# Seven block products for eight in the up projection of a hybrid decoder layer

## The chip, the cores and the metric

The kernel runs on one core of a Trainium2 chip. The metric is the device time of one launch in microseconds. Engines are named as in the profile: PE (TensorE, matrix products), DVE (VectorE), ACT (ScalarE), POOL (GpSimd) and SP (which only issues DMAs here).

## The reference, cut to what matters

One decoder layer for 576 tokens: a prompt of 512 and eight sequences of 8 sample tokens. The width is 1024, the hidden width of the MLP 4096, all in float32.

```python
hn = rmsnorm(x, norm1_g)
proj = hn @ w_in                    # split between the two mixers
...                                 # gated DeltaNet (oa) and dilated attention (ob)
h1 = x + jnp.concatenate([oa, ob], axis=-1) @ w_o
hid = jnp.square(jax.nn.relu(rmsnorm(h1, norm2_g) @ w_up))
y = h1 + hid @ w_down
```

`rmsnorm` divides each token by the root of its mean square and multiplies by a gain per channel. The change concerns the last two lines and the residual that leads to them.

## The kernel before

Activations lie with channels on the 128 partitions and tokens along the free dimension, so the layer's input is 8 channel tiles of 576 tokens. The tokens are handled in two halves of 288.

**Products in two parts.** Each operand of a large product is split into a rounded value (`h`, in the type fp32r that PE takes at full rate) and a remainder (`l`). A product is then three: wh·xh, wh·xl and wl·xh, added in one PSUM bank. A weight chunk of 128 x 1024 is loaded (`wr`), ACT writes `wh`, and DVE subtracts to get `wl` (`splitter`, line 397).

**Stages.** First the attention projections, attention and delta rule run, interleaved. Then comes the output projection (`proj_o`, line 1532), in two halves of the contraction: the attention's half first (tile `mob`), then the delta heads' half (tile `moa`). For each of the 8 channel tiles `m` and each token half, `after_o` (line 1505) adds the result to the residual `h1`, writes `h1 * gain` in two parts (`h1h`, `h1l`) and squares it; POOL adds the squares up. When all squares are there, `stats2` sums them over the partitions with five small products into `ssum`, and spreads the scale of each token over the partitions (`row_bcast`: PE transposes into `rowb`, ACT copies out).

**MLP.** The blocks go in the order u0, u1, d0, u2, d1, ... u7, d6, d7. A block u makes 512 hidden channels: four row tiles, each a product over 8 channel tiles for both token halves. `relu2` takes it out of PSUM with two DVE operations (the token's scale is applied there, so the products don't wait for it), and splits the square in two parts (`hid`). A block d multiplies 512 hidden channels by w_down, and `add_down` adds each result to `h1`.

**What sets the order.** All of this is written as generators. `Flow` (line 91) merges them into one program order by a rough clock of its own for each engine; each engine then runs its instructions strictly in that order. What a generator needs is given by signals (`yield lambda: "delta" in done`) and by buffer classes with a limit (`get`, `rel`); the four classes share fixed numbers of tiles, `K` 13 of 1024 columns and `P` the 8 PSUM banks. `proj_o` and `mlp_gemm` are fillers: PE takes their next product whenever nothing else of PE's can start sooner.

Of the kernel before, what the change touches and what calls it, by code (L numbers as in the profile page):

```python
# [11 lines left out]
F32R = mybir.dt.float32r  # L12
# [5 lines left out]
NT = SEQ + NB * TS          # 576 tokens: the prompt, then the sample batches one after another  # L18
# [51 lines left out]
_GROUP = {"sb": "cs", "sbn": "cs", "pb": "cf"}     # the rest: "c"; parameters: "cp"  # L70
# [20 lines left out]
class Flow:  # L91
    """A list scheduler: merges generators into one program order, by a rough clock of each engine.
    A generator's instructions wait in its queue, and the one that can start first is issued.
    What a generator brings in one step is in order, and what follows a yield depends on it; one
    that fills has steps that depend on nothing but the times it is given. A generator yields a
    further delay, or a test that has to hold before its next step."""
# [4 lines left out]
    AHEAD = 4000      # how far loads that can wait may queue up  # L101
# [62 lines left out]
    def advance(self, c):  # L164
        """to the task's next instruction, if it has one yet"""
# [47 lines left out]
def hymba_step(ctx: ExitStack, tc: tile.TileContext, a):  # L213
# [5 lines left out]
    # a few classes of buffers, each shared by several uses; those that are held are counted, so  # L219
    # that none waits for a release that comes later in program order  # L220
# [36 lines left out]
    def mm(out, lhsT, rhs, start, stop, share=1):  # L257
        n = size(rhs) * (1 if rhs.dtype == F32R else 4)
        cost = max(n, size(lhsT) * (1 if rhs.dtype == F32R else 4)) / 2.4 + 3
# [63 lines left out]
    go_on = lambda t: None      # mark of what nothing in the generator waits for  # L323
# [13 lines left out]
    klass(kpool, "K", 13, {"wr": WR, "wh": 2, "wl": 2, "kv": 1, "es": 2, "so": 2, "ex": 3, "k": 13, "e": 2})  # L337
    klass(upool, "U", 16, {"st": 2, "nat": 7, "sq": 2, "cv": 4, "E": 1, "t": 6, "h1": 8, "rq": 4, "u": 16})
# [34 lines left out]
    for kind, c in order:  # L373
        for i in range(4):
            chunk[kind, c, i] = len(items)
            items.append((a["wu"][4 * c + i] if kind == "u" else a["wd"][c, i], 1024))
    raw = {}

    def load_w(i):
        src, cols = items[i]  # L380
        r = yield from get("wr", MID, "wr")
        dma(r[:, :cols], src, lambda t: raw.update({i: (r, t)}))
# [139 lines left out]
    # q and k of the prompt in two parts; the heads' outputs take the place of the lower parts  # L522
# [36 lines left out]
    def first_products(ps, n):  # L559
        """of the first chunk: each kind of product once its parts are there"""  # L560
# [340 lines left out]
    def gemm(wh, wl, x_h, x_l, nk, stride, off, after, need=None):  # L901
        """w^T x over nk tiles of the contraction, by halves of the tokens; after(half, psum) has
        the generator that takes a half away."""
        for hf, (c0, c1) in enumerate(HALF):
            p = yield from get("g", [128, 288], "pg")
            for j in range(nk):
                s = slice(j * stride + off, j * stride + off + 128)
                if need and need(j, hf) not in done:
                    yield lambda: need(j, hf) in done
                mm(p, wh[:, s], x_h[:, j, c0:c1], j == 0, False)  # L910
                mm(p, wh[:, s], x_l[:, j, c0:c1], False, False)
                mm(p, wl[:, s], x_h[:, j, c0:c1], False, j == nk - 1)
# [166 lines left out]
    def head_decay(h):  # L1079
        """the decay between tokens of a chunk, in either direction"""  # L1080
# [19 lines left out]
    def head_scores(h):  # L1100
        """k k^T and q k^T with the decay between tokens; the former goes to DRAM"""
# [70 lines left out]
    def head_tokens(h):  # L1172
        """k and v with tokens on partitions"""
# [40 lines left out]
    def substitution(nb, n, src, buf):  # L1214
        """Inverse of the unit lower triangular blocks src (one per partition), and its transpose."""
# [27 lines left out]
    def sub_prompt():  # L1243
# [16 lines left out]
        # the blocks of twice the size: a pair on two partitions, with half of the columns each  # L1260
# [222 lines left out]
    def after_delta():  # L1483
# [3 lines left out]
        rel("big")  # L1487
        cap.update(g=6, wr=4, wh=3, wl=3)
        sig("delta")

# [14 lines left out]
    def after_o(m, hf, p, last):  # L1505
# [9 lines left out]
        g = C["g2"][:, m:m + 1]  # L1515
        xh_ = hx["h"][:, m, c0:c1]
        yield 0
        act(xh_, x, scale=g)
        stt(hx["l"][:, m, c0:c1], x, g, f(xh_), OP.mult, OP.subtract)
        sig(("h1", m, hf))  # L1520
        yield 0
        acc = st2["acc"]
        if m:
            s = yield from get("t", [128, 288], "sq2")
            act(s, x, AF.Square)
            pool_tt(acc[:, c0:c1], acc[:, c0:c1], s, OP.add)
            rel("t")
        else:
            act(acc[:, c0:c1], x, AF.Square)
        sig(("sq", m, hf))  # L1530

    def proj_o():
        yield lambda: "prompt_attn" in done and "sample_attn" in done
        for kh in (1, 0):
            if kh:
                x = mob["t"]
            else:
                yield lambda: "delta" in done
# [11 lines left out]
        rel("big", "big")  # L1550
        sig("proj_o")
# [183 lines left out]
```

## Time and profile before

| | us |
|---|---|
| median of 3 runs | 830.47 |
| lowest and highest run | 829.9, 831.32 |
| span of the profiled execution, first to last instruction | 830.0 |

The profile is of one execution. Its page gives the span and no other time for that execution. Busy time of an engine is the time in which it executes an instruction. Lines such as L262 or L278 are helpers (`mm`, `tt`) through which all matrix products and all two-input DVE operations go, so the tiles tell them apart. A name before `<-` is what is written, those behind it are what is read.

### The profile page before, as it was taken

To read this page: it belongs to the slowest core of one execution; us is meant where nothing else is said; L and a number is where in the kernel's file an instruction comes from. 1 tells how busy PE (TensorE), PEld (TensorE's weight loads), DVE (VectorE), ACT (ScalarE), POOL (GpSimd) and SP (SyncE) were. 2 spreads that over 40 slices of the span, in tenths; PEclk is the share of its full clock that TensorE was granted. 3 is DMA by queue.
4 is the path that set the end of the run, shared out by engine and by line. 5 is a ranking of instruction groups with operands and counts; after the bars stand their busy time and mean duration, and the time that the engine had idled before them with its cause. 6 is when DMAs were issued, how large, how long until landed. Compare 5 with 4: busy or idle time off the path is not lost.

```text
span 830.0 us, 15794 instructions
## 1 busy us (share of the span) xinstructions
PE 811.8 (98%) x6486; PEld 750.2 (90%) x6486; DVE 506.3 (61%) x1126; ACT 283.8 (34%) x594; POOL 121.9 (15%) x140
## 2 busy tenths in 40 slices
PE   9989998999999999999999999999999999999998
PEld 9968877879778787789999999999999999999998
DVE  4366279788776885688756545546455554645552
ACT  5547454554332244442633212222132121222210
POOL 3443323134223000040520000000000000000000
PEclk9999999999999999999999999999999999999999
DMA  7722421016787896224223222222322232222102
GB/s 266 134 99 77 135 69 37 29 40 231 236 313 217 296 312 258 86 82 176 86 69 102 77 77 87 92 77 77 99 81 77 77 101 78 77 81 96 54 28 87
DMA packets 49863, 99.05 MB, mean 119 GB/s; under 512 B 12864, under 2 KB 26304, under 8 KB 49792
## 3 DMA queue, kind: packets, MB, share of 16 engines
q1 hardware_dynamic: 49792, 98.05, 35.9%
q8 instruction: 51, 0.84, 0.4%
q14 instruction: 20, 0.16, 0.1%
HBM read 88.15 MB, written 9.69 MB: 118 GB/s over the span
## 4 chain that ended last, share of the span: by engine, by line
PE 83%; DVE 8%; DMA 3%; ACT 3%; issue 1%; POOL 0%; SPq 0%; ACTq 0%; POOLq 0%
PE pg L262 61%; PE pa L262 8%; DVE y L285 3%; PE cha L262 2%; DMA wr<-in_wk_dram 1%; DMA morekv<-in_cv_dram 1%; PE ptp L265 1%; PE sn L262 1%; PE os L262 1%; PE sc L262 1%; PE cs L262 1%; PE py L262 1%; PE pv L262 1%; PE s L262 1%; ACT wh L270 1%
## 5 line engine op out<-in xcount | busy, mean ns | idle before, releaser
L262 PE MATMUL pg<-hid,wh 128*128 128x288 f32 x1024 | 203.7, 294 | 0.0
L262 PEld LDWEIGHTS pg<-hid,wh 128*128 128x128 f32 x1024 | 164.3, 188 | 0.0
L262 PE MATMUL pg<-h1h,wl 128*128 128x288 f32 x512 | 151.2, 295 | 0.0
L262 PE MATMUL pg<-hid,wl 128*128 128x288 f32 x512 | 151.2, 295 | 0.0
L262 PE MATMUL pg<-h1l,wh 128*128 128x288 f32 x512 | 150.9, 295 | 0.0
L262 PE MATMUL pg<-h1h,wh 128*128 128x288 f32 x512 | 150.7, 294 | 0.0
L270 ACT ACTIVATE wh<-wr 128x1024 fp32r<-128x1024 f32 (+1 forms) x104 | 105.7, 1017 | 110.2 <-PE pg L262 72.1
L278 DVE TENSOR_TENSOR h<-pg,h 128x288 f32<-128x288 f32 x160 | 72.9, 457 | 114.1 <-PE pg L262 114.1
L278 DVE TENSOR_TENSOR wl<-wr,wh 128x1024 fp32r<-128x1024 f32 (+1 forms) x89 | 107.1, 1203 | 16.2 <-ACT wh L270 16.0
L262 PEld LDWEIGHTS pg<-h1l,wh 128*128 128x128 f32 x512 | 96.1, 188 | 0.1
L262 PEld LDWEIGHTS pg<-h1h,wl 128*128 128x128 f32 x512 | 96.1, 188 | 0.0
L262 PEld LDWEIGHTS pg<-hid,wl 128*128 128x128 f32 x512 | 96.1, 188 | 0.0
L262 PEld LDWEIGHTS pg<-h1h,wh 128*128 128x128 f32 x512 | 96.1, 188 | 0.0
L270 ACT ACTIVATE hid<-rq 128x288 fp32r<-128x288 f32 x64 | 28.5, 445 | 181.5 <-DVE rq L285 181.5
L262 PE MATMUL pg<-xh,wh 128*128 128x288 f32 x256 | 78.3, 306 | 0.0
L262 PE MATMUL pg<-xh,wl 128*128 128x288 f32 x256 | 78.2, 305 | 0.0
L262 PE MATMUL pg<-xl,wh 128*128 128x288 f32 x256 | 78.1, 305 | 0.0
L285 DVE SCALAR_TENSOR_TENSOR rq<-pg,R2b 128x288 f32<-128x288 f32 x64 | 29.3, 458 | 68.4 <-PE pg L262 66.5
L262 PEld LDWEIGHTS pg<-xh,wh 128*128 128x128 f32 x256 | 48.6, 190 | 3.2 <-issue 3.0
L262 PEld LDWEIGHTS pg<-xh,wl 128*128 128x128 f32 x256 | 48.7, 190 | 2.8 <-issue 2.4
L262 PEld LDWEIGHTS pg<-xl,wh 128*128 128x128 f32 x256 | 48.7, 190 | 2.5 <-issue 1.8
L308 POOL TENSOR_TENSOR wl<-wr,wh 128x1024 fp32r<-128x1024 f32 x15 | 35.9, 2393 | 83.0 <-ACT wh L270 66.5
(281 smaller groups left out, 1331.2 us busy)
## 6 DMA issues: line engine op xcount, KB each, us to landing
wr<-in_wu_dram SPq DMA_DIRECT2D x32, 512.0 KB, 3.2
wr<-in_wd_dram SPq DMA_DIRECT2D x32, 512.0 KB, 3.3
morekv<-in_ck_dram SPq DMA_DIRECT2D x20, 512.0 KB, 4.9
morekv<-in_cv_dram SPq DMA_DIRECT2D x20, 512.0 KB, 5.8
wr<-in_wb_dram SPq DMA_DIRECT2D x16, 512.0 KB, 4.0
wr<-in_wo_dram SPq DMA_DIRECT2D x8, 512.0 KB, 5.5
xr<-in_xT_dram SPq DMA_DIRECT2D x8, 288.0 KB, 5.3
h<-in_xT_dram SPq DMA_DIRECT2D x8, 288.0 KB, 6.8
```

What stands on the lines that cost most here:

```text
L262: lambda: nc.tensor.matmul(out, lhsT, rhs, start=start, stop=stop, skip_group_check=True))
L265: fl.op("PE", (97, 230), lambda: nc.tensor.transpose(out, in_, ident[:k, :k]))
L270: fl.op("ACT", cost, lambda: nc.scalar.activation(out, in_, func, bias=bias, scale=scale, accum_out=accum), mark)
L278: dve(lambda: nc.vector.tensor_tensor(out, x, y, op=op), out, x, mark=mark)
L285: dve(lambda: nc.vector.scalar_tensor_tensor(out, x, s, y, op0=op0, op1=op1), out, x, 61 if ap(s) else 0, mark=mark)
L308: fl.op("POOL", 135 + size(x) / 0.47, lambda: nc.gpsimd.tensor_tensor(out, x, y, op=op), mark)
```

## The change

The product with w_up is made in blocks of 2 x 2: a unit is a pair of row tiles (256 hidden channels, 16 units in all), the contraction goes over four pairs of channel tiles, and the tokens are the two halves. A product of two 2 x 2 block matrices takes eight block products; written with sums of the blocks of either factor (Winograd's form of Strassen's scheme), it takes seven. Each of the seven has a PSUM bank of its own for the whole unit.

- Weights: a chunk now holds half the contraction of a pair of row tiles. POOL forms three sums (`ws`, 768 columns) and overwrites a quarter of the chunk by a fourth combination, in operations of 256 columns (`sums_splitter`). ACT and DVE then split both tiles in two parts (`two_parts`).
- Inputs: `after_o` writes `h1 * gain` in single precision into `xq`. POOL multiplies it by a scale S per token, from the first norm's variances, and forms four combinations (`x_factors`); ACT and DVE split the seven results (`x_parts`, tiles `xf`). S is spread by `token_scale`, and the second half of `proj_o` waits for it. The second norm's scale (`stats2`) divides S out again.
- Outputs: `up_out` forms the four blocks of the result from the seven banks, one operation on ACT and seven on DVE per unit, in `uq`; `up_square` applies the norm's scale, squares and splits.

`PO` is the order of the seven products; `OF_W` and `OF_X` name the factor of each. The long list of buffer limits is left out of the diff.

```diff
-            items.append((a["wu"][4 * c + i] if kind == "u" else a["wd"][c, i], 1024))
+            if kind == "u":
+                m, k = 4 * c + i // 2 * 2, i % 2 * 512
+                items.append((a["wu"][m:m + 2, :, k:k + 512].rearrange("m p k -> p m k"), 1024))
+            else:
+                items.append((a["wd"][c, i], 1024))
...
+    def sums_splitter():
+        yield lambda: "S" in done
+        for i in range(MLP, len(items)):
...
+                pool_tt(S1, A21, A22, OP.add)
+                pool_tt(A21, A11, A21, OP.subtract)
+                pool_tt(S2, S1, A11, OP.subtract)
+                pool_tt(S4, A12, S2, OP.subtract)
+                fl.spawn(two_parts(i, r, s))
...
+    def two_parts(i, r, s):
...
+        for x, n, uh, ul in ((r, 1024, "mh", "ml"), (s, 768, "mg", "mm")):
...
+                act(h[:, :n], x[:, :n])
...
+            tt(l[:, :n], x[:, :n], f(h[:, :n]), OP.subtract)
...
         yield lambda: all(("out", c) in done for c in range(5))
-        rel("big")
-        cap.update(g=6, wr=4, wh=3, wl=3)
+        rel("big", "big")
+        st2["S"] = yield from get("k", [128, NT], "S")
...
+        cap.update(g=6, wr=3, wh=3, wl=3)
...
-        act(xh_, x, scale=g)
-        stt(hx["l"][:, m, c0:c1], x, g, f(xh_), OP.mult, OP.subtract)
+        act(hx[i].q[2 * hf + m % 2], x, scale=C["g2"][:, m:m + 1])
...
+    def x_factors(i):
...
+        for hf in range(2):
+            yield lambda: all(("z", 2 * i + j, hf) in done for j in range(2))
+            pool_tt(x.two(hf), x.two(hf), both(st2["S"], hf), OP.mult)
+        yield 0
+        pool_tt(q[4], q[2], q[0], OP.subtract)
+        fl.spawn(x_parts(i, (0, 1)))
+        pool_tt(q[5], q[3], q[4], OP.subtract)
+        pool_tt(q[2], q[3], q[2], OP.subtract)
+        fl.spawn(x_parts(i, (2, 3)))
+        pool_tt(q[6], q[5], q[1], OP.subtract)
+        fl.spawn(x_parts(i, (4, 5, 6)))
...
+    def x_parts(i, js):
...
+            act(h[:, c], x.t[j // 2][:, :n])
+            yield 0
+            tt(l[:, c], x.t[j // 2][:, :n], f(h[:, c]), OP.subtract)
...
+    def token_scale():
+        yield lambda: "delta" in done
+        ts(sc1, var1, 1.0, None, OP.add)
+        recip(ims1, sc1)
+        pow_m_half(sc1, sc1, 5)
+        yield 0
+        yield from row_bcast(st2["S"], sc1)
+        sig("S")
...
-                yield lambda: "delta" in done
+                yield lambda: "S" in done
...
-        recip(R2, R2)
+        tt(R2, R2, ims1, OP.mult)
+        pow_m_half(R2, R2, 5)
         yield 0
-        yield from row_bcast(st2["R"], R2)
+        yield from row_bcast(st2["S"], R2)
...
+    def up(u):
+        P = {}
+        fl.spawn(up_square(u))
+        for kk in range(2):
+            w = yield from take(chunk["u", u // 2, u % 2 * 2 + kk])
+            for p in PO:
+                if not kk:
+                    P[p] = yield from get("g", [128, 288], "pg")
...
+                    mm(P[p], wh[:, s], xh_, k == 0, False, extra=8)
+                    mm(P[p], wh[:, s], xl_, False, False, extra=8)
+                    mm(P[p], wl[:, s], xh_, False, k == 3, extra=8)
...
+                if kk:
+                    fl.spawn(up_out(u, p, P[p]))
...
+    def up_out(u, p, P):
...
+        if p == 1:
+            act(q[4], P)
+        elif p == 4:
+            tt(q[1], q[6], P, OP.subtract)
+        else:
+            if p == 5:
+                tt(q[3], P, q[6], OP.add)
+            o, i = {2: (0, 4), 6: (5, 4), 7: (6, 5), 5: (5, 5), 3: (2, 5)}[p]
+            tt(q[o], P, q[i], OP.add)
...
+    def up_square(u):
...
-        stt(r, p, 0.0, st2["R"][:, c0:c1], OP.max, OP.mult)
-        stt(q, p, 0.0, r, OP.max, OP.mult)
-        rel("g")
-        act(hid[c][:, 0, i, c0:c1], q)
-        tt(hid[c][:, 1, i, c0:c1], q, f(hid[c][:, 0, i, c0:c1]), OP.subtract)
...
+            stt(d, d, 0.0, both(st2["S"], hf), OP.max, OP.mult)
+            act(d, d, AF.Square)
+            act(hid[c][:, 0, r, c0:c1], d)
+            tt(hid[c][:, 1, r, c0:c1], d, f(hid[c][:, 0, r, c0:c1]), OP.subtract)
```


The order of all engines is the same up to the last part of the output projection, but for S. Three places where it moves follow.

POOL, at the end of the output projection, before: the last steps of the delta heads (`so`, `ro`), and then to the end only squares (`sq`, one per channel tile and half) that are added to `acc`.

```order
L308 TENSOR_TENSOR so<-so,eGLs 128x1024 [waits DMAHW3_49,DMAHW2_49,DMAHW7_49,PE_49,Activation_49]
L317 TENSOR_TENSOR ro<-vo,neghalf 128x4 [waits DVE_49]
L317 TENSOR_TENSOR ro<-vo,neghalf 64x4 [waits DVE_49]
L317 TENSOR_TENSOR ro<-vo,neghalf 128x4 [waits DVE_49]
L308 TENSOR_TENSOR acc_4528<-acc_4528,sq_4598 128x288 [waits PE_49,Activation_49]
L308 TENSOR_TENSOR acc_4528<-acc_4528,sq_4634 128x288 [waits Activation_49]
L308 TENSOR_TENSOR acc_4528<-acc_4528,sq_4655 128x288 [waits Activation_49,Pool_49]
```

The same place after, the last part of it: `xq` are the inputs and their combinations for the third and the fourth pair of channel tiles (pair numbers differ by the buffer number), `acc2` the sum of squares, `S` the scale.

```order
L308 TENSOR_TENSOR xq_4769<-xq_4769,S_4464 128x576 [waits Activation_49]
L308 TENSOR_TENSOR acc2_4465<-acc2_4465,sq2_4466 128x288
L308 TENSOR_TENSOR xq_4770<-xq_4770,S_4464 128x576 [waits Activation_49]
L308 TENSOR_TENSOR acc2_4465<-acc2_4465,sq2_4466 128x288
L308 TENSOR_TENSOR xq_4771<-xq_4770,xq_4769 128x288 [waits DVE_49,Pool_49]
L308 TENSOR_TENSOR xq_4771<-xq_4770,xq_4771 128x288 [waits Pool_49]
L308 TENSOR_TENSOR xq_4770<-xq_4770 128x288
L308 TENSOR_TENSOR xq_4772<-xq_4771,xq_4769 128x288 [waits DVE_49,Pool_49]
L308 TENSOR_TENSOR xq_4890<-xq_4890,S_4464 128x576 [waits Activation_49]
L308 TENSOR_TENSOR acc2_4465<-acc2_4465,sq2_4466 128x288
L308 TENSOR_TENSOR xq_4891<-xq_4891,S_4464 128x576 [waits Activation_49]
L308 TENSOR_TENSOR acc2_4465<-acc2_4465,sq2_4466 128x288
```

Between the additions of squares now stand the scaling and the combinations of each pair of channel tiles; in front of these rows are those of the first two pairs and three of the weight chunks' sums, and behind them the last six squares with one more chunk's sums among them.

PE, where the sums of squares are taken over the partitions (`ssum`), before: this is late in the first row tile of block u0.

```order
L262 MATMUL pg<-h1h,wl 128x288
L262 MATMUL pg<-h1h,wh 128x288
L262 MATMUL pg<-h1l,wh 128x288
L262 MATMUL ssum<-c,acc_4528 128x1 [waits Pool_49]
L262 MATMUL ssum<-c,acc_4528 128x1
L262 MATMUL ssum<-c,acc_4528 128x1 [waits Pool_49]
L262 MATMUL ssum<-c,acc_4528 128x1
L262 MATMUL ssum<-c,acc_4528 64x1
L262 MATMUL pg<-h1h,wl 128x288
L262 MATMUL pg<-h1h,wh 128x288
```

And after: `xf` are the input's factors; the six products in front of `ssum` (three of them shown) belong to the second unit.

```order
L262 MATMUL pg<-xf_4543,wh 128x288
L262 MATMUL pg<-xf_4545,wh 128x288
L262 MATMUL pg<-xf_4543,wl 128x288
L262 MATMUL ssum<-c,acc_4465 128x1 [waits Pool_49]
L262 MATMUL ssum<-c,acc_4465 128x1
L262 MATMUL ssum<-c,acc_4465 128x1 [waits Pool_49]
L262 MATMUL ssum<-c,acc_4465 128x1
L262 MATMUL ssum<-c,acc_4465 64x1
L262 MATMUL pg<-xf_4543,wh 128x288
L262 MATMUL pg<-xf_4545,wh 128x288
```

The five small products still wait for POOL. Ahead of them stand the whole first unit (84 products, on all four pairs' factors) and six products of the second, instead of products on `h1h` and `h1l`.

DVE, in the first two blocks u, before: `rq` is the result of a row tile on its way to `hid`, `wl` the remainder of a weight chunk.

```order
L285 SCALAR_TENSOR_TENSOR rq<-pg,rq 128x288
L278 TENSOR_TENSOR hid<-rq,hid 128x288
L285 SCALAR_TENSOR_TENSOR rq<-pg,R2b 128x288
L285 SCALAR_TENSOR_TENSOR rq<-pg,rq 128x288
L278 TENSOR_TENSOR wl<-wr,wh 128x1024
L278 TENSOR_TENSOR hid<-rq,hid 128x288
L285 SCALAR_TENSOR_TENSOR rq<-pg,R2b 128x288
```

And after, at the end of the second unit: `uq` are the sums of the second unit's banks, and the `wl` in the last row but two is the first chunk of the third unit.

```order
L278 TENSOR_TENSOR uq<-pg,uq 128x288 x2
L278 TENSOR_TENSOR uq<-uq,pg 128x288
L285 SCALAR_TENSOR_TENSOR uq<-uq,S 128x576
L278 TENSOR_TENSOR hid<-uq,hid 128x2x288
L278 TENSOR_TENSOR uq<-pg,uq 128x288 x3
L278 TENSOR_TENSOR hid<-uq,hid 128x2x288
L278 TENSOR_TENSOR wl<-wr,wh 128x1024
L285 SCALAR_TENSOR_TENSOR uq<-uq,S 128x576
L278 TENSOR_TENSOR wl<-ws,wh 128x768
```

A weight chunk was split between two row tiles' results; the third unit's first chunk is split behind all sums of the second unit.

## Rows read from the trace of the kernel before

**Rows 1.** Busy time of each engine over the whole span (us, share, instructions)
```profile
PE 811.8 (98%) x6486; PEld 750.2 (90%) x6486; DVE 506.3 (61%) x1126; ACT 283.8 (34%) x594; POOL 121.9 (15%) x140
```

**Rows 2.** Chain of waits that ended last: start us, us, engine, tile, line, pieces
```profile
383.81 38.41 PE pg L262 x290
425.90 400.76 PE pg L262 x3023
```

**Rows 3.** Stretches: from:to, us, busy us of PE, PEld, DVE, ACT, POOL; granted clock, DMA share, GB/s
```profile
600.00:700.00 100.00, 100.00 (x757) 100.00 (x756) 52.71 (x96) 22.98 (x32) 0.00 (x0) 1.00 0.26 85
```

**Rows 4.** Tile moa: duration ns min/median/max, first and last start us, forms
```profile
L262 PE MATMUL pg<-moa,wh x128: 288/295/297, 392.0 to 417.2; 128*128 128x288 f32 x128
...
L278 DVE TENSOR_TENSOR moa<-on,moa x5: 419/678/682, 361.4 to 386.2; 128x512 fp32r<-128x512 f32 x4, 128x256 fp32r<-128x256 f32 x1
```

**Rows 5.** Timeline, GpSimd, 385 to 430: start us, us, instruction, [idle before <-releaser]
```profile
399.35 2.50 POOL L308 TENSOR_TENSOR acc<-acc,sq 128x288 f32<-128x288 f32 x2 [25.35 <-ACT sq L270]
403.25 1.57 POOL L308 TENSOR_TENSOR acc<-acc,sq 128x288 f32<-128x288 f32 x2 [1.40 <-ACT sq L270]
405.77 2.81 POOL L308 TENSOR_TENSOR acc<-acc,sq 128x288 f32<-128x288 f32 x2 [0.96 <-ACT sq L270]
```

**Rows 6.** Groups by shape, GpSimd: xcount | busy us, mean ns | idle before
```profile
L308 POOL TENSOR_TENSOR acc<-acc,sq 128x288 f32<-128x288 f32 x14 | 15.5, 1129 | 31.8 <-ACT sq L270 31.8
...
L308 POOL TENSOR_TENSOR acc<-acc,sq 128x576 f32<-128x576 f32 x7 | 10.2, 1450 | 8.7 <-ACT sq L270 8.7
...
L317 POOL TENSOR_TENSOR rs<-var,neghalf 128x5 f32<-128x5 f32 x1 | 1.2, 1185 | 6.5 <-DVE var L282 6.5
```

**Rows 7.** Timeline, GpSimd, 24 to 34
```profile
25.12 1.43 POOL L308 TENSOR_TENSOR acc<-acc,sq 128x576 f32<-128x576 f32 x1 [0.80 <-ACT sq L270]
```

**Rows 8.** Timeline, VectorE, 14 to 34
```profile
22.28 0.70 DVE L278 TENSOR_TENSOR wl<-wr,wh 128x520 fp32r<-128x520 f32 x1
25.60 1.51 DVE L278 TENSOR_TENSOR wl<-wr,wh 128x520 fp32r<-128x520 f32 x1 [2.62 <-ACT wh L270]
```

**Rows 9.** Timeline, VectorE, 385 to 430
```profile
405.29 0.51 DVE L285 SCALAR_TENSOR_TENSOR h1l<-h,cp,h1h 128x288 fp32r<-128x288 f32 x1
405.72 1.22 DVE L278 TENSOR_TENSOR wl<-wr,wh 128x1024 fp32r<-128x1024 f32 x1
406.86 1.06 DVE L285 SCALAR_TENSOR_TENSOR h1l<-h,cp,h1h 128x288 fp32r<-128x288 f32 x1
```

**Rows 10.** Groups by shape, VectorE, 430 to 830
```profile
L278 DVE TENSOR_TENSOR wl<-wr,wh 128x1024 fp32r<-128x1024 f32 x60 | 72.9, 1216 | 0.0
L278 DVE TENSOR_TENSOR h<-pg,h 128x288 f32<-128x288 f32 x128 | 58.6, 458 | 105.8 <-PE pg L262 105.8
L278 DVE TENSOR_TENSOR hid<-rq,hid 128x288 fp32r<-128x288 f32 x63 | 28.7, 455 | 15.3 <-ACT hid L270 15.3
```

**Rows 11.** Groups by shape, VectorE, 0 to 430
```profile
L285 DVE SCALAR_TENSOR_TENSOR silvz<-y,silvz 128x576 f32<-128x576 f32 x4 | 3.0, 750 | 0.0
```

**Rows 12.** Groups by shape, ScalarE, 425 to 830
```profile
L270 ACT ACTIVATE wh<-wr 128x1024 fp32r<-128x1024 f32 x61 | 64.1, 1050 | 100.0 <-PE pg L262 72.1 <-issue 27.2 <-DVE wl L278 0.6
L270 ACT ACTIVATE hid<-rq 128x288 fp32r<-128x288 f32 x64 | 28.5, 445 | 181.5 <-DVE rq L285 181.5
L270 ACT ACTIVATE R2b<-rowb 128x512 f32<-128x512 f32 x1 | 0.6, 598 | 5.6 <-PE rowb L265 5.6
```

**Rows 13.** What TensorE waited for: us in total, times, longest us
```profile
PE rowb L265 <- POOL rs L317: 2.3, 1, 2.3
```

**Rows 14.** Stretches, 28 to 48
```profile
28.00:34.00 6.00, 6.00 (x53) 6.00 (x52) 3.63 (x3) 4.29 (x10) 3.78 (x3) 1.00 1.19 148
...
44.00:45.00 1.00, 1.00 (x6) 0.91 (x6) 0.96 (x7) 0.49 (x1) 0.38 (x1) 0.68 0.02 4
...
46.00:47.00 1.00, 1.00 (x4) 0.36 (x3) 0.62 (x2) 0.12 (x2) 1.00 (x2) 0.50 0.78 143
...
48.00:49.00 1.00, 1.00 (x7) 0.77 (x7) 0.97 (x3) 0.00 (x0) 1.00 (x1) 1.00 1.01 414
```

More of the change, by code (lines that the diff above doesn't have):

```diff
@@ L255, in hymba_step, with mm @@
     ap = lambda x: not isinstance(x, (int, float))
-    def mm(out, lhsT, rhs, start, stop, share=1):
+    def mm(out, lhsT, rhs, start, stop, share=1, extra=0):
         n = size(rhs) * (1 if rhs.dtype == F32R else 4)
-        cost = max(n, size(lhsT) * (1 if rhs.dtype == F32R else 4)) / 2.4 + 3
+        cost = max(n, size(lhsT) * (1 if rhs.dtype == F32R else 4)) / 2.4 + 3 + extra
         cost = cost if share == 1 else cost / share + 15
@@ L380, in load_w @@
         src, cols = items[i]
-        r = yield from get("wr", MID, "wr")
-        dma(r[:, :cols], src, lambda t: raw.update({i: (r, t)}))
+        r = yield from get("wr" if i < MLP else "mr", MID, "wr")
+        d = r[:, :cols]
+        if len(src.shape) == 3:
+            d = d.rearrange("p (m k) -> p m k", m=src.shape[1])
+        dma(d, src, lambda t: raw.update({i: (r, t)}))
     def loader():
@@ L899, in hymba_step, with gemm @@
     UW = 604
-    def gemm(wh, wl, x_h, x_l, nk, stride, off, after, need=None):
+    def gemm(wh, wl, x_h, x_l, nk, stride, off, after, extra=0):
         for hf, (c0, c1) in enumerate(HALF):
@@ L907, in gemm @@
                 s = slice(j * stride + off, j * stride + off + 128)
[L908 to L912, printed above, removed]
+                mm(p, wh[:, s], x_h[:, j, c0:c1], j == 0, False, extra=extra)
+                mm(p, wh[:, s], x_l[:, j, c0:c1], False, False, extra=extra)
+                mm(p, wl[:, s], x_h[:, j, c0:c1], False, j == nk - 1, extra=extra)
                 yield 0
@@ L1523, in after_o @@
         if m:
-            s = yield from get("t", [128, 288], "sq2")
+            n = 2 * m + hf
+            last = [("sq", m - 1, hf)] + [("sq", (n - 3) // 2, (n - 3) % 2)] * (n >= 5)
+            if not all(x in done for x in last):
+                yield lambda: all(x in done for x in last)
+            n = n % 3 * 288
+            s = st2["sq"][:, n:n + 288]
             act(s, x, AF.Square)
             pool_tt(acc[:, c0:c1], acc[:, c0:c1], s, OP.add)
-            rel("t")
         else:
@@ L1554, in stats2 @@
         yield lambda: all(("sq", m, hf) in done for m in range(8) for hf in range(2))
+        yield lambda: all(("xf", i) in done for i in range(4))
         p = yield from token_sums(st2["acc"])
@@ new lines, in up_out @@
+    def up_out(u, p, P):
+        after = ("q", u) if p == 1 else ("up", u, {2: 1, 6: 1, 7: 6, 4: 7, 5: 7, 3: 5}[p])
+        if after not in done:
+            yield lambda: after in done
+        q = Q[u].q
+        if p == 1:
+            act(q[4], P)
+        elif p == 4:
+            tt(q[1], q[6], P, OP.subtract)
+        else:
+            if p == 5:
+                tt(q[3], P, q[6], OP.add)
+            o, i = {2: (0, 4), 6: (5, 4), 7: (6, 5), 5: (5, 5), 3: (2, 5)}[p]
+            tt(q[o], P, q[i], OP.add)
+        rel("g")
+        yield 0
+        sig(("up", u, p))
@@ new lines, in up_square @@
+    def up_square(u):
+        x = Q[u] = yield from quad("uq")
+        sig(("q", u))
+        yield lambda: "R2b" in done
+        c, r = u // 2, slice(u % 2 * 2, u % 2 * 2 + 2)
+        for hf, need in ((0, (2, 4)), (1, (5, 3))):
+            if not all(("up", u, p) in done for p in need):
+                yield lambda: all(("up", u, p) in done for p in need)
+            d = x.two(hf)
+            c0, c1 = HALF[hf]
+            stt(d, d, 0.0, both(st2["S"], hf), OP.max, OP.mult)
+            act(d, d, AF.Square)
+            act(hid[c][:, 0, r, c0:c1], d)
+            tt(hid[c][:, 1, r, c0:c1], d, f(hid[c][:, 0, r, c0:c1]), OP.subtract)
+            sig(("hid", u, hf))
+            yield 0
+        rel("q", "q", "q", "q")
```

142 lines of the change are left out of this document (112 added, 30 removed).

## The prediction

> **What bounds the kernel now.** I read the engine lines first: TensorE is busy 98% of the span, VectorE 61%, GpSimd 15% [rows 1]. The chain of waits then says where the end is made: from 383.81 us on it is TensorE alone, 38.41 us and then 400.76 us of one group of products [rows 2]; nothing waits there. In that stretch 757 products of 288 columns start per 100 us, 132.1 ns each, at the full granted clock, with VectorE at 53% and GpSimd idle [rows 3]. So in the second half a product taken away is 132.1 ns, as long as nobody else becomes late. The change touches only this half: up to the output projection the order of every engine is the same.
>
> **What it removes.** The product with w_up has 32 row tiles x 8 x 2 halves x 3 = 1536 matmuls before; after, 16 pairs x 2 x 7 x 6 = 1344. 192 x 0.1321 = **-25.4 us**, if TensorE keeps its pace.
>
> **The added scale S.** The second half of the output projection now waits for S, which is asked for only after the last delta head. The last moa part ends at 386.2 + 0.68 = 386.9 us [rows 4]; two small VectorE operations (estimate 0.4 from their sizes) and one power on GpSimd, 1.19 us [rows 6], bring it to 388.6. In the order its five transposes stand 26 products ahead of the first moa product, at 392.0 - 26 x 0.1321 = 388.5. That is a wait near zero (0.4 for handovers) and 0.5 for five small matmuls: **+0.9 us**, 0.5 to 2.8 (the 2.3 us that the same step cost at its first use [rows 13]). The moa products then start at 392.9.
>
> **GpSimd at the passage into the MLP.** This is the term that decides. Before, GpSimd adds 14 squares there, 15.5 us of work in all [rows 6]. Now it scales the inputs (8 operations of 576), forms the combinations of inputs (16 of 288), adds the squares (14 of 288) and sums three weight chunks (12 of 256; a fourth chunk, done first, is over before the first input comes), all in one queue. TensorE's order then holds the five ssum products, six matmuls into the second unit, and they wait for the last square, which stands behind all 50.
> Durations: two 288 alone take 1.57, so 0.785 each [rows 5]; 576 alone 1.43 [rows 7]; 256 is not in the trace, 0.71 on the line through these two. Sum 8 x 1.43 + 30 x 0.785 + 12 x 0.71 = 11.4 + 23.6 + 8.5 = 43.5 us. Start: the first square now reaches GpSimd 7.4 us after the moa start (399.35 against 392.0) [rows 4, 5]; the first scaling needs the same tile, without the square (0.445 for that size on ScalarE) and the part of a 1.05 us weight copy in front of it there [rows 12], so 6.2 us after 392.9: 399.1. Alone, GpSimd would finish at 442.6.
> It isn't alone. A split of 520 columns that takes 0.70 took 1.51 when it started 0.48 us into a GpSimd addition: it ended 0.7 after that one's end [rows 7, 8]. The other way too: a pair of additions beside a 1.22 us split took 2.81 for 1.57, and the 0.51 us step behind that split took 1.06 [rows 5, 9]. So an operation of VectorE that reads two SBUF tensors and one of GpSimd take turns. VectorE puts these between GpSimd's 50: 12 differences of 576 (0.75 [rows 11]), 4 of 288 (0.455), 5 splits of 1024 (1.216) [rows 10] and 3 of 768 (0.93, by size): 9.0 + 1.8 + 6.1 + 2.8 = 19.7. GpSimd's fixed part of an operation, 0.14 us by the two sizes above, runs beside; 24 x 0.14 = 3.4 off. 399.1 + 43.5 + 16.3 = **458.9**. A second way gives nearly the same: at the 1.129 us that a 288 took on average in just this stretch [rows 6], in proportion for 256 and at 1.45 for 576, the 50 take 57.8, to 456.9. I take 458.9, from the rows that show the turns one by one.
> TensorE without a wait would be at ssum at 392.9 + (192 + 84 + 6) x 0.1321 = 430.2. So it stands for **+28.7 us** in pieces (for the last wo split, for combinations of pairs two to four, then ssum). The bounds are +12.4 (no turns) and +32 (turns with nothing beside). It was hidden before because only the 0.785 us additions stood ahead of ssum; the cover is gone because the combinations must be ready before a product can use them.
>
> **The first units after that.** At the third unit the weights come late: in VectorE's order their split stands behind the second unit's last sums. From ssum on, S of the second norm takes 1.19 + 0.6 us and handovers [rows 6, 12], about 4.3; then VectorE has 6 operations of 576 (4.5), 7 of 288 from PSUM (3.2) [rows 10, 11] and the split (1.2): 13.2 us after ssum, 15 with the waits for ScalarE's squares in between. TensorE needs it after 78 products, 10.6 us. **+4 us**, and +1 for the eighth chunk in the same manner; 1 to 9 together.
>
> **The clock.** After a wait of 2.3 us for GpSimd [rows 13] the granted clock was below full between 44 and 48 us, 0.50 in the middle, which is the level of 1.2 GHz, and 1.00 again from 48: at most 2 us lost [rows 14]. The waits here are longer, but what is lost during them is hidden; only a slow start behind ssum counts: **+1**, 0 to 3.
>
> **The steady cycle.** Two units and one w_down block are 360 products, 47.6 us. VectorE: 8 splits of 1024, 4 of 768, 14 sums, 16 additions from PSUM, 8 operations of 576: 9.7 + 3.7 + 6.4 + 7.3 + 6.0 = 33.1 us; GpSimd 16 x 0.71 = 11.4. Even taking turns throughout, 44.5, this fits, and 8 PSUM banks for 7 products leave each sum six products of time. ScalarE stays under half. The weight chunks are read in 2 KB pieces instead of 4 KB, at a quarter of the DMA's share [rows 3]. I take 0, up to +10 by the rival below.
>
> **Sum.** -25.4 + 0.9 + 28.7 + 5 + 1 = +10.2 on the span of 830.0, 840.2. The page gives no time beyond the span for this execution; the median of the runs, 830.47, lies 0.5 above it: **840.7 us**.
>
> A rule weighed. In the rows, matmuls that change the PSUM bank at each step, in the first projection, ran 53 in 6 us with the clock at 1.00 [rows 14], so a change of bank every six products should cost nothing here. The Trainium skill, "TensorE: Matmul & The Clock Gate", section "A second HAM failure mode: psum-queue depth-cycling", says that cycling through PSUM banks makes TensorE idle briefly so often that its clock swings between the two levels. By the rows the sum stays; by that rule it would gain a part of 1344 x 0.13 us (the half level takes twice as long): rival 3.
>
> **Rivals.** 1. GpSimd and VectorE hardly hold each other up, because VectorE's operations fall into gaps: GpSimd ends between 442.6 and 447.1 (the 4.5 us by which 15.5 exceeds 14 x 0.785 [rows 5, 6]). The wait is 12.4 to 16.9, what follows costs 5 as the clock then hardly falls, and the result is -7.1 to -2.6: 823.4 to 827.9 us, faster. For it: the rows show turns only at a load under which GpSimd was idle for a quarter of the time [rows 5]. Against: now both queues are full. It decides from an end at 448.7, where the sum is zero. Chance 0.23.
> 2. VectorE becomes the bound of the steady cycle: 44.5 of 47.6 us leaves little, and two units in a row pack 20 us of VectorE into 22. At 1.4 us late per cycle, seven cycles: +10, 851 us. Against: the w_down half of each cycle has slack, and weights are split a block ahead. Chance 0.13.
> 3. The bank rule: were a tenth of the up products at the lower level, 134 x 0.13 = +18 on my sum, 858 us. Against it the row above. Chance 0.02.
> That the matmuls don't go away is excluded: they are gone from the order.
>
> **Chances.** My forecast 0.60, rival 1 0.23, rival 2 0.13, rival 3 0.02, anything else 0.02. A measurement of this kernel can tell 0.2%, 1.7 us. Faster: rival 1 and a little of the rest, 0.24. Same: ends of GpSimd between 447 and 450.5, 0.05. Slower 0.71. The range takes in the upper part of rival 1 and rival 2: 825 to 852; my own case alone has 832 to 847.
>
> **What would show it.** Right: TensorE's group for the up products with 1344 matmuls; GpSimd busy without a pause for some 60 us from 399, its 288s near 1.1 us on average; TensorE mostly idle between 431 and 449 and again at ssum until about 459, with the clock at half in between; a wait of some 4 us for a weight split at the third unit; then an even 132 ns. Wrong: ssum released near 443, or waits of TensorE for VectorE in each later cycle, or a pace of the products other than 132 ns.

## The result, and the profile after

The changed kernel took **837.15 us** (median of 4 runs, 836.51 to 839.0), the kernel before 830.89 beside it (829.9 to 832.1): a ratio of 1.0086, 95% interval 1.0065 to 1.0106. It is slower by 6.3 us. The forecast was 840.7 us, slower. The profiled execution took 836.92 us with a span of 835.1. In the experiments below some executions, of the kernel before as well, took 845 to 858 us at a lower granted clock (0.95 to 0.97 on average), and their medians leave these out.

The engine lines (us busy, share, instructions), to set beside [rows 1]:
```profile
PE 794.9 (95%) x6299; PEld 730.8 (88%) x6299; DVE 569.1 (68%) x1144; ACT 342.0 (41%) x660; POOL 276.2 (33%) x294
```
TensorE has 187 matmuls less (192 products gone, 5 transposes of S added) and is busy 16.9 us less; the span is 5.1 us longer. The products with w_up are now 896 + 448 = 1344 (groups):
```profile
L262 PE MATMUL pg<-xf,wh 128*128 128x288 f32 x896 | 183.9, 300 | 8.0 <-DVE xf L278 7.8
L262 PE MATMUL pg<-xf,wl 128*128 128x288 f32 x448 | 134.5, 300 | 9.5 <-DVE wl L278 9.5
```
The chain of waits (start us, us, engine, tile, line, pieces), where [rows 2] had TensorE alone from 383.81 on:
```profile
431.72 2.15 POOL xq L308 x2
435.13 2.35 POOL xq L308
440.29 4.08 POOL xq L308 x3
444.37 2.35 POOL acc L308 x2
...
469.20 1.23 DVE wl L278
470.47 361.31 PE pg L262 x2710
```
Ahead of the MLP the chain now runs over GpSimd to 453.7, then in short steps over all engines, the last of them on VectorE at 469.20, and from 470.47 on it is TensorE again to the end. The stretches of 10 us (columns as in [rows 3]) show the same:
```profile
400.00:410.00 10.00, 10.00 (x78) 10.00 (x77) 7.78 (x8) 5.97 (x13) 9.92 (x9) 1.00 0.18 53
410.00:420.00 10.00, 6.45 (x28) 5.98 (x27) 6.10 (x9) 4.15 (x9) 9.76 (x10) 0.67 0.01 2
420.00:430.00 10.00, 9.49 (x69) 9.05 (x67) 5.10 (x7) 5.20 (x11) 9.84 (x10) 0.99 0.00 0
430.00:440.00 10.00, 1.21 (x2) 0.57 (x2) 7.49 (x5) 5.24 (x9) 9.92 (x9) 0.69 0.00 1
440.00:450.00 10.00, 4.96 (x20) 4.96 (x21) 8.97 (x9) 3.44 (x8) 9.84 (x10) 0.50 0.19 52
450.00:460.00 10.00, 9.40 (x68) 8.96 (x67) 4.92 (x11) 2.39 (x3) 7.09 (x9) 0.95 0.33 107
460.00:470.00 10.00, 7.34 (x53) 6.97 (x52) 8.19 (x14) 7.54 (x12) 5.55 (x6) 1.00 0.15 50
470.00:480.00 10.00, 9.53 (x60) 9.54 (x61) 7.62 (x8) 4.19 (x6) 6.55 (x7) 0.83 0.19 57
...
600.00:700.00 100.00, 100.00 (x756) 100.00 (x755) 68.96 (x104) 36.11 (x45) 33.57 (x36) 1.00 0.27 85
```
Read the last busy column first: GpSimd has no pause from 400 to 450. TensorE falls from 78 products per 10 us to 28, 2 and 20 in three of the next four stretches, and behind its long waits its clock is at the half level (1.2 GHz; 0.50 from 440 to 450, a mixture of both levels in the stretches with 0.67, 0.69 and 0.83). From 480 on it is 756 products per 100 us, 132.3 ns each, against 132.1 before.

TensorE's idle times in that passage (timeline: start us, us, instruction, [idle before <-releaser]):
```profile
412.68 0.53 PE L262 MATMUL pg<-moa,wh 128*128 128x288 f32 x2 [2.32 <-ACT wh L270]
414.45 0.61 PE L262 MATMUL pg<-moa,wl 128*128 128x288 f32 x1 [1.24 <-DVE wl L278]
...
436.28 0.61 PE L262 MATMUL pg<-xf,wl 128*128 128x288 f32 x1 [6.33 <-DVE wl L278]
...
445.04 0.61 PE L262 MATMUL pg<-xf,wh 128*128 128x288 f32 x1 [7.35 <-DVE xf L278]
...
453.62 1.15 PE L262 MATMUL ssum<-c,acc 128*128 128x1 f32 x10
...
458.35 0.65 PE L265 MATMUL rowb<-c,R 128*128 128x128 f32 x4 [0.59 <-POOL R L317]
...
470.47 0.40 PE L262 MATMUL pg<-xf,wl 128*128 128x288 f32 x1 [3.13 <-DVE wl L278]
```
The releasers named are mostly VectorE's splits; GpSimd is named for 0.59 us alone, and ssum waits for nothing. A releaser is only the last link: the xf split behind the 7.35 us needs ScalarE's upper part, and that needs GpSimd's combinations. What ScalarE waited for, 386 to 480 (us in total, times, longest us):
```profile
ACT xf L270 <- POOL xq L308: 15.6, 4, 6.4
```

GpSimd's operations in that passage (groups by shape, 392 to 480), to set beside [rows 6]:
```profile
L308 POOL TENSOR_TENSOR xq<-xq 128x288 f32<-128x288 f32 x16 | 17.8, 1129 | 0.3
L308 POOL TENSOR_TENSOR acc<-acc,sq 128x288 f32<-128x288 f32 x14 | 15.0, 1083 | 0.0
L308 POOL TENSOR_TENSOR xq<-xq,S 128x576 f32<-128x576 f32 x8 | 13.6, 1696 | 2.0 <-ACT xq L270 2.0
```
And why they are so long, in one place. VectorE:
```profile
434.41 1.81 DVE L278 TENSOR_TENSOR wl<-wr,wh 128x1024 fp32r<-128x1024 f32 x1
436.14 2.16 DVE L278 TENSOR_TENSOR wl<-ws,wh 128x768 fp32r<-128x768 f32 x1
```
and GpSimd in the same microseconds:
```profile
433.83 1.30 POOL L308 TENSOR_TENSOR acc<-acc,sq 128x288 f32<-128x288 f32 x1
435.10 2.39 POOL L308 TENSOR_TENSOR xq<-xq,S 128x576 f32<-128x576 f32 x1
437.45 1.50 POOL L308 TENSOR_TENSOR acc<-acc,sq 128x288 f32<-128x288 f32 x1
```
Each operation begins while the other engine's runs, stands until that one ends, and then takes 0.13 to 0.16 us less than its time alone: 434.41 waits for the end at 435.13 and takes 1.1 more (1.22 alone); 435.10 waits for 436.22 and takes 1.3 more (1.43 alone); 436.14 waits for 437.49, 437.45 for 438.30. Here they go strictly in turn. The Trainium skill, "SBUF — State Buffer", section "Who interferes with whom", says that a VectorE instruction with two SBUF inputs contends with a GpSimd instruction that reads SBUF, that the shared ports are an exclusive lock, and that the order of issue decides who blocks; these rows agree.

### The profile page after: what moved, and what is told of

It is laid out like the page before. It is cut to its first block, busy times and chain, and to the rows that moved or that the text cites. A ratio compares the mean times of both kernels' runs of the same rounds, so it can differ in the third digit from the quotient of the medians.

```text
span 835.1 us, 15803 instructions
## 1 busy us (share of the span) xinstructions
PE 794.9 (95%) x6299; PEld 730.8 (88%) x6299; DVE 569.1 (68%) x1144; ACT 342.0 (41%) x660; POOL 276.2 (33%) x294
## 4 chain that ended last, share of the span: by engine, by line
PE 72%; POOL 8%; DVE 7%; issue 5%; DMA 4%; ACT 3%; SPq 2%; POOLq 0%; ACTq 0%; DVEq 0%
PE pg L262 52%; PE pa L262 7%; POOL xq L308 3%; SPq L321 2%; POOL acc L308 2%; PE cha L262 2%; DVE y L285 2%; DMA morekv<-in_ck_dram 1%; DMA wr<-in_wk_dram 1%; PE os L262 1%; POOL ws L308 1%; PE ptp L265 1%; PE sc L262 1%; PE cs L262 1%; PE s L262 1%
## 5 line engine op out<-in xcount | busy, mean ns | idle before, releaser
L262 PE MATMUL pg<-xf,wh 128*128 128x288 f32 x896 | 183.9, 300 | 8.0 <-DVE xf L278 7.8
L262 PEld LDWEIGHTS pg<-xf,wh 128*128 128x128 f32 x896 | 147.3, 192 | 9.0 <-DVE xf L278 8.3
L262 PE MATMUL pg<-xf,wl 128*128 128x288 f32 x448 | 134.5, 300 | 9.5 <-DVE wl L278 9.5
L278 DVE TENSOR_TENSOR wl<-wr,wh 128x1024 fp32r<-128x1024 f32 (+1 forms) x89 | 116.6, 1311 | 27.2 <-ACT wh L270 26.7
L308 POOL TENSOR_TENSOR ws<-wr 128x256 f32<-128x256 f32 x32 | 28.8, 900 | 203.5 <-DMA wr<-in_wu_dram 101.2
L262 PEld LDWEIGHTS pg<-xf,wl 128*128 128x128 f32 x448 | 86.1, 192 | 9.9 <-DVE wl L278 9.9
L278 DVE TENSOR_TENSOR uq<-pg,uq 128x288 f32<-128x288 f32 x96 | 42.2, 454 | 15.6 <-PE pg L262 13.7
L270 ACT ACTIVATE uq<-uq 128x576 f32<-128x576 f32 x32 | 22.0, 686 | 61.7 <-DVE uq L285 61.6
L270 ACT ACTIVATE wh<-ws 128x768 fp32r<-128x768 f32 x32 | 26.9, 840 | 45.6 <-POOL ws L308 17.5
```

What stands on the lines that cost most here:

```text
L262: lambda: nc.tensor.matmul(out, lhsT, rhs, start=start, stop=stop, skip_group_check=True))
L270: fl.op("ACT", cost, lambda: nc.scalar.activation(out, in_, func, bias=bias, scale=scale, accum_out=accum), mark)
L278: dve(lambda: nc.vector.tensor_tensor(out, x, y, op=op), out, x, mark=mark)
L308: fl.op("POOL", 135 + size(x) / 0.47, lambda: nc.gpsimd.tensor_tensor(out, x, y, op=op), mark)
```

## The experiments

To take out the few us by which the first half differs from one execution to another (the first w_o product of the second half starts at 391 to 395 us in the same order), the profiles are compared from that start to the end of the span: 438.0 before, 444.0 after. "Lost" is the time from that start to ssum, less 0.1321 for each product in between: 25.2 us in the changed kernel (453.62 - 391.13 - 282 x 0.1321). "Rest" is the time from ssum to the end, less 0.1321 for each product left, less the 6.8 that before has outside its products: 6.2 (381.53 - 2790 x 0.1321 - 6.8). These figures come from one profile of each kernel. Ratios are to the kernel before, measured on the same chip (831.2 to 831.8).

**Combinations and scaling on VectorE.**
```
-            pool_tt(x.two(hf), x.two(hf), both(st2["S"], hf), OP.mult)
+            tt(x.two(hf), x.two(hf), both(st2["S"], hf), OP.mult)
-        pool_tt(q[4], q[2], q[0], OP.subtract)
+        tt(q[4], q[2], q[0], OP.subtract)
...
```
(q[5], q[2] and q[6] in the same way.)


> The 8 scalings by S and the 16 combinations of inputs go from GpSimd to VectorE; GpSimd keeps the squares and the weight sums. Theory (GpSimd's queue of 50 operations makes the wait at the passage, 25 us): its queue there falls to 26 operations, about 19.5 us alone, and ends well before 440; VectorE takes 8 x 0.75 + 16 x 0.455 = 13.3 us more and is then the longer one, with about 43 us of work from 397 on, to 440 at the worst where TensorE could be at 428. So 10 to 20 us less than the changed kernel: 817 to 827 us. Rival (VectorE is the real brake, as the longest waits of TensorE name its splits): 13.3 us more on it lengthen the passage, 845 to 850 us.


Measured: **826.11 us** (8 runs), ratio 0.9934 [0.9913, 0.9955]; 431.2 from the start on, 12.8 less than the changed kernel; lost 17.0, rest 1.6. The theory holds: the time is in its range and 19 us below the rival's, with more work on the engine that the waits name.

**Scaling fused with the gain on VectorE.**
```
-        act(hx[i].q[2 * hf + m % 2], x, scale=C["g2"][:, m:m + 1])
+        stt(hx[i].q[2 * hf + m % 2], x, C["g2"][:, m:m + 1], st2["S"][:, c0:c1], OP.mult, OP.mult)
...
-            pool_tt(x.two(hf), x.two(hf), both(st2["S"], hf), OP.mult)
```


> The scaling by S is done in the step that multiplies by the gain (one VectorE operation of 288 in place of ScalarE's scaled copy of 288 and half a GpSimd operation of 576); the combinations stay on GpSimd. Theory (GpSimd's queue): 8 operations at 1.70 us, 13.6 us, leave it, and the passage ends about 12 us earlier: 823 to 828 us. Rival (VectorE is the brake): 16 x 0.5 = 8 us more on it, 843 to 846 us.


Measured: **827.82 us** (7 runs), ratio 0.9958 [0.9936, 0.998]; 432.6, lost 16.5, rest 3.5. The theory holds, at the upper end of its range.

**Lower parts of the inputs left out.**
```
-            tt(l[:, c], x.t[j // 2][:, :n], f(h[:, c]), OP.subtract)
...
-                    mm(P[p], wh[:, s], xl_, False, False, extra=8)
+                    mm(P[p], wh[:, s], xh_, False, False, extra=8)
```


> Leaves out the lower parts of the input combinations (VectorE's 16 differences of 576 and 288 are not made; their products read the upper part instead). GpSimd's operations are all kept. If GpSimd and VectorE take turns, taking 12 x 0.75 + 4 x 0.455 = 10.8 us of VectorE's two-input work out of the passage lowers GpSimd's mean for 288 there from 1.11 to about 0.95 us and ends its queue 6 to 11 us earlier (443 to 448 instead of 453.7): 826 to 832 us. Rival (GpSimd is as slow as that by itself): its means stay at 1.1 and 1.7, its queue ends at 453 as before, and the time changes by less than 3 us.


Measured: 829.17 us (one run). GpSimd's groups by shape, with not one of its operations changed:
```profile
L308 POOL TENSOR_TENSOR xq<-xq,S 128x576 f32<-128x576 f32 x8 | 13.9, 1733 | 2.0 <-ACT xq L270 2.0
L308 POOL TENSOR_TENSOR xq<-xq 128x288 f32<-128x288 f32 x16 | 13.6, 870 | 0.3
L308 POOL TENSOR_TENSOR acc<-acc,sq 128x288 f32<-128x288 f32 x14 | 12.8, 923 | 0.0
```
The combinations fell from 1.129 to 0.870 us and the squares from 1.083 to 0.923. GpSimd's 50 operations took 49.6 us (398.98 to 448.6) for 56.5, 43.5 being their time alone: about half of the turn-taking came from these 16 splits. Lost falls to 17.7. The theory holds, in the range of its time and in an end that is 6.9 us earlier, counted from the first w_o product; that GpSimd is slow by itself is refuted. VectorE is less than half busy here, and GpSimd all the time (columns as in [rows 3]):
```profile
400.00:440.00 40.00, 31.33 (x197) 30.06 (x195) 17.71 (x20) 22.29 (x43) 39.37 (x39) 0.85 0.09 27
```

**Splits of the w_up and w_down chunks earlier in the order.**
```
-                fl.spawn(two_parts(i, r, s))
+                fl.spawn(two_parts(i, r, s), "w")
```
The w_down chunks' line in the same way; the new bias is w=-2000.


> The weight splits of the MLP stand earlier in the order of ScalarE and VectorE, ahead of sums and squares that are ready at the same time. Theory (the 3.1 us wait at the third unit, with 1.6 us of half clock behind it, comes from the split standing behind the second unit's sums): that wait goes, 831 to 834 us. Rival (the split can't come earlier, since its buffers come free only with the second unit's first half): the same wait stays, or comes back as a wait for a PSUM bank, 836 to 839 us.


Measured: 840.75 us (one run); 444.7 from the start on, against 444.0. The wait at the third unit falls from 3.1 to 1.1, but the waits for xf in the passage grow (10.6 us for 7.8):
```profile
441.70 0.61 PE L262 MATMUL pg<-xf,wh 128*128 128x288 f32 x1 [5.04 <-DVE xf L278]
...
446.12 0.61 PE L262 MATMUL pg<-xf,wh 128*128 128x288 f32 x1 [2.10 <-DVE xf L278]
...
474.23 0.40 PE L262 MATMUL pg<-xf,wl 128*128 128x288 f32 x1 [1.08 <-DVE wl L278]
```
The wait could be moved, but nothing was won; neither expectation is met as written.

**GpSimd's cost in the scheduler times 1.4.**
```
+        slow = 1.4 if "delta" in done else 1.0
-        fl.op("POOL", 135 + size(x) / 0.47, ...
+        fl.op("POOL", slow * (135 + size(x) / 0.47), ...
```


> The changed kernel with only the scheduler's cost of a GpSimd operation raised by 1.4 from the last delta head on, near what the traces show: the same instructions in another order (ssum stands after 303 products instead of 282). Theory (the work of GpSimd and VectorE on two-input operations is what fills the passage): that work is the same, so the passage keeps its length within 3 us: 834 to 839 us. Rival (the loss is one of order, made because the scheduler takes GpSimd's operations as standing alone): the passage shortens by 7 us or more, below 830 us.


Measured: **842.32 us** (4 runs), ratio 1.0101 [1.0061, 1.0142]; lost 27.1. An order made with truer costs is no better; it is 3.5 us worse from the start on (447.5 for 444.0). The rival falls, and the size was outside what the theory gave.

**Everything of the inputs on VectorE** (the fused scaling, the combinations on VectorE and the factor 1.4 together).


> Fused scaling and the 16 combinations on VectorE; GpSimd keeps squares and weight sums; GpSimd's cost in the scheduler as before times 1.4. Theory (two-input operations of both engines share one path, so their times add whichever engine has them): 16 combinations at 0.455 instead of 0.785 us take 5 us off the common work: 3 to 6 us less than with the fused scaling alone, 822 to 825 us. Rival (the engines' own queues count, and VectorE is the longer): 7.3 us more on VectorE, 833 to 836 us.


Measured: **826.46 us** (5 runs), ratio 0.9922 [0.9891, 0.9953]; 432.8, lost 15.7, rest 4.5. The time lies between the two expectations: not the 3 to 6 us less than the fused scaling that the common path alone would give, nor the rival's 6 more. The factor 1.4, which cost the changed kernel 3.5 us by itself, is in it too, so what the combinations alone do isn't separated. The stretch from 400 to 440 us (columns as before) shows who is busy. The changed kernel:
```profile
400.00:440.00 40.00, 27.15 (x173) 25.60 (x171) 26.47 (x28) 20.57 (x39) 39.45 (x35) 0.84 0.05 14
```
combinations and scaling on VectorE:
```profile
400.00:440.00 40.00, 29.62 (x197) 28.57 (x195) 38.52 (x55) 26.06 (x50) 25.77 (x22) 0.89 0.04 14
```
fused scaling:
```profile
400.00:440.00 40.00, 28.28 (x183) 27.47 (x182) 37.73 (x45) 18.27 (x35) 37.39 (x35) 0.84 0.04 14
```
all on VectorE:
```profile
400.00:440.00 40.00, 29.20 (x193) 28.39 (x193) 39.83 (x62) 19.68 (x37) 22.45 (x21) 0.88 0.05 15
```
In the changed kernel GpSimd is busy 39.5 of 40 us and VectorE 26.5. In the three others VectorE is at 38 to 40. By these shares VectorE takes over as the bound after some 11 us; that is a reading of busy time, and no run tests it by itself.

**Squares later in the order; and with the w_o splits first.**
```
+        fl.spawn(square(m, hf, x), "sq")
...
+            fl.spawn(splitter(hi, MLP), "wo")
```
Both contain the fused scaling. The first line, with a bias sq=1500, is in both; the second, a splitter of its own for the w_o chunks with a bias wo=-3000, in the latter. In these and the next three orders one signal also has a new name (`"Q"` for `"q"`), which an earlier part of the kernel had in use.


> Fused scaling on VectorE, and the squares and their sums stand later in the order, so that GpSimd makes the combinations first and ssum comes after 338 products instead of 256. Theory: the additions of squares (14 of 288) leave the time in which the products wait; 3 to 7 us less than with the fused scaling alone, 821 to 825 us. Rival (the same wait comes back behind the second unit, where the second norm's scale is then late): 826 to 830 us.

> As the one with the squares later, and the splits of the w_o chunks stand ahead of what is ready at the same time, so that they don't stand behind splits of inputs that wait for GpSimd. Theory: the two waits of TensorE for the last w_o chunk (3.4 and 3.7 us, and the half clock after them) go: 2 to 6 us less than with the squares later alone, 816 to 822 us. Rival (VectorE is busy throughout there, so what is moved forward makes the inputs late instead): within 2 us of it.


Measured: 835.27 us (9 runs), ratio 1.0036 [1.0005, 1.0067], and 830.92 (9 runs), ratio 0.9986 [0.9963, 1.0008]. Both are slower than the fused scaling alone, and the first is above both of its expectations. The w_o splits first bring some 4 us here, within the theory's 2 to 6, but not to the time that it gave. The first, at ssum and behind it:
```profile
459.00 2.16 PE L262 MATMUL ssum<-c,acc 128*128 128x1 f32 x10 [3.70 <-POOL acc L308]
475.66 0.61 PE L262 MATMUL pg<-xf,wl 128*128 128x288 f32 x1 [2.68 <-DVE wl L278]
```
Ssum, though it stands 82 products later, now does wait for the squares, and the rest grows to 7.7. Putting them behind moved the wait to a place with less cover.

**The w_o splits first, squares in their place**: with the fused scaling, with everything on VectorE, and that with the splits of the first two w_up chunks early too. (Both of the latter have the factor 1.4.)


> Fused scaling on VectorE (combinations on GpSimd), and the splits of the w_o chunks stand ahead of what is ready at the same time. Theory (after the unloading of GpSimd, VectorE is the passage's bound: from 400 to 443 us it is busy almost without a pause): the waits for the last w_o chunk go (3.4 and 3.7 us, and half clock behind them), but only what VectorE's own pauses of 1.5 and 0.5 us there and GpSimd's earlier start give is won: 823 to 828 us. Rival (those waits are a loss of their own): 6 us or more below the fused scaling alone, 818 to 822 us.

> All input operations on VectorE, as before, and the w_o splits first. Theory (VectorE's work is the bound): VectorE has no pause between 404 and 443 us to fill, but 2 to 3 us before 404; 822 to 826 us. Rival (the waits for the last w_o chunk, 4.2 and 2.0 us with half clock behind them, are a loss of their own): 817 to 821 us.

> As the one with all input operations on VectorE and the w_o splits first; the splits of the first two w_up chunks are also put ahead of what is ready at the same time. Theory (VectorE's work is the bound, and it has some 3 us of pauses before 404 us that the first chunk's split, 1.22 + 0.94 us, can fill): 1 to 3 us less than without it, 820 to 824 us. Rival (the splits only push the inputs back): the same or up to 3 us more, 823 to 828 us.


Measured: 829.86 (9 runs, 0.9986 [0.9962, 1.001]), 828.1 (7 runs, 0.9959 [0.9932, 0.9985]) and 832.35 us (10 runs, 1.0005 [0.9984, 1.0025]). The second's profile is of an execution of 851.42 us and isn't read for the passage. In the first, the waits for the last w_o chunk are gone and others stand in their place:
```profile
428.64 0.61 PE L262 MATMUL pg<-xf,wh 128*128 128x288 f32 x1 [2.41 <-DVE xf L278]
431.57 0.61 PE L262 MATMUL pg<-xf,wl 128*128 128x288 f32 x1 [2.32 <-DVE wl L278]
435.56 0.61 PE L262 MATMUL pg<-xf,wh 128*128 128x288 f32 x1 [3.15 <-DVE xf L278]
```
The rival (these waits are a loss of their own) is refuted; the gains that the theory allowed (up to 5 us) didn't come either: by the ratios each is some 2 to 4 us above the kernel that it changes, and the third, which was to be 1 to 3 below the second, is some 4 above it. No kernel here is below the 826 us of the first and of the one with all on VectorE, which both beat the kernel before.

## Why the prediction was right

| step | forecast | measured | from |
|---|---|---|---|
| products gone | -25.4 | -25.4 | 1344 matmuls at 132.3 ns |
| S | +0.9 | +1.9 | last moa part to first moa product: 5.8 before, 7.7 after |
| GpSimd at the passage | +28.7 | +25.2 | lost |
| first units, clock | +5 and +1 | +6.2 | rest |
| sum | +10.2 | +7.9 | |
| first half | 0 | -2.8 | last moa part at 383.4, before 386.2 |

7.9 - 2.8 is the 5.1 of the spans. The 2.8 is chance: in the eight profiles with the same order up to there the last moa part starts between 383.4 and 387.6. The 0.5 us taken for what lies outside the span was too small: in every other execution of the kernel before it is 2.2 to 2.3, and 1.8 in the changed one. So the profile before is probably of an execution of some 832 us, above the median, and the spans make the change look smaller than the medians, which differ by 6.3 for the forecast's 10.2. The forecast came within 3.6 us of the time partly by luck: GpSimd's -3.5 and S's +1.0 take each other off, and so do the first half's -2.8 and the 1.3 that were missing outside the span.

*GpSimd.* The mechanism was right: a queue of 50 operations without a pause, lengthened by VectorE. It took 56.5 us (397.2 to 453.7) for the 59.8 of the forecast: the turns cost 13.0, not 16.3. That term was oversized by a quarter, and this is nearly all of the 3.5 us between 28.7 and 25.2. One of the five splits of 1024 that it counts came only behind GpSimd's end (at 454.83), which is 1.1 of the 3.3; the rest isn't explained. Its row for the turns was read a little high too: the split of 520 columns ended 0.56 us after the addition (25.60 + 1.51 against 25.12 + 1.43), not 0.7. The unloading experiments show the cause (17.0 and 16.5 lost for 25.2), leaving out the lower parts shows the turns. Rival 1 asked for an end by 447.1; with an end at 453.7 it fails, and even with VectorE's 16 input splits taken out GpSimd ended 55.7 us after the first w_o product (448.6 - 392.9), where rival 1 needed 54.2 (447.1 - 392.9).

*Where TensorE waits.* The forecast had a last wait at ssum until GpSimd's end. There is none: TensorE reached ssum at 453.62, when GpSimd's last addition was about to end (453.71). Of the 25.2 us, 17.9 are idle time in six pieces, and 5.7 are products at the half clock (412.7 to 420 and 445 to 451); the rest is mostly the few products that stand alone between two waits. The forecast took such slow products as hidden by the waits; that held in sum, because they stood in the place of the wait at ssum.

*S.* The wait was 0.8 us for GpSimd's power, which took 2.09 us where 1.19 was taken from its first use. That is the forecast's own mechanism at a place where the forecast did not look for it. In the changed kernel the power begins 0.16 us into a weight split on VectorE:
```profile
384.35 1.23 DVE L278 TENSOR_TENSOR wl<-wr,wh 128x1024 fp32r<-128x1024 f32 x1
384.51 2.09 POOL L317 TENSOR_TENSOR sc<-sc,neghalf 128x5 f32<-128x5 f32 x1 [13.30 <-DVE ims L295]
```
It ends 1.02 us after the split does (386.60 against 385.58). In the fused scaling with the w_o splits first, that split is over before the power begins:
```profile
386.67 1.22 DVE L278 TENSOR_TENSOR wl<-wr,wh 128x1024 fp32r<-128x1024 f32 x1
388.27 1.17 POOL L317 TENSOR_TENSOR sc<-sc,neghalf 128x5 f32<-128x5 f32 x1 [15.60 <-DVE ims L295]
```
The power takes 2.09 us in all eight profiles with the first order and 1.16 or 1.17 in the four with the w_o splits first.

*First units and clock.* One wait at the third unit (3.1), 0.6 for the second norm's power, some 1.6 of products at the lower clock (22 in 4.5 us from 470.5 on), and about 0.5 over the 2650 products from 480 on at 132.3 ns for 132.1: 5.8 of the 6.2. The wait was forecast as 4; its 78 products are 10.3 us, where the forecast has 10.6. The wait forecast for the eighth chunk didn't come: behind 480 us TensorE waits for nothing.

*Rivals 2 and 3.* VectorE is busy 69 of 100 us in the steady cycle, the forecast's 33.1 of 47.6 (70%), and no wait appears: rival 2 is out. Rival 3 is out as well: the clock is 1.00 there with a change of bank every six products. The row given against it was misread in one point: those matmuls of the first projection change the bank every six as well (every four for the sample tokens), not at each step, so it was the same case and not a harder one. The rule of the Trainium skill, "TensorE: Matmul & The Clock Gate", section "A second HAM failure mode: psum-queue depth-cycling", has nothing to act on here, since TensorE doesn't pause between the groups: it is busy 100.00 of 100 us.

*What stays open.* The w_up saving is 25.4 us and the best kernel here keeps about 6 of it. In the best kernels 16 or 17 us stay lost, and VectorE is busy almost without a pause; that less work on it would then free TensorE was not tried. With the lower parts left out VectorE was busy 17.7 of 40 us and as much was lost (17.7), but there GpSimd still had all its 50 operations. None of the orders tried on top of the unloading helped. Why truer costs make a worse order is not explained either.

## What to carry to other kernels

When work is moved off the busiest engine, add up the other engines' queues in the stage where the consumer must wait for them, not over the span: GpSimd was at 33% overall and at 99% where it mattered. Two-input operations of VectorE and GpSimd on SBUF take turns, so a schedule that counts them side by side is too short; raising GpSimd's costs in the scheduler, though, did not give a better order here. And a list of waits names the last link: here it said VectorE, and unloading GpSimd is what helped.

## What the runs showed of the hardware that was not expected

The turns are whole operations, in both directions: a 768-column split of 0.95 us took 2.16, a 576 on GpSimd of 1.43 took 2.39. Even a power of 5 columns on GpSimd takes its turn: S's 2.09 us where a split of 1024 began 0.16 us before it, and 1.16 or 1.17 where none did; the second norm's 1.82 or 1.83 us in the two profiles where a split of 768 began 0.16 us before it, and 1.18 in the other ten. In identical order the first half of the program took 391 to 395 us in eight profiles.
